# Experts' output rows: scattered to DRAM by token and choice and added once at the end, instead of added set by set through a one-hot product

## The chip, the cores and the metric

The kernel runs on one core of one Trainium2 chip. The core has TensorE (PE, matrix products into PSUM), VectorE (DVE), ScalarE (ACT), GpSimd (Pool) and SyncE (SP), each with its own queue of instructions, and 16 DMA engines that all queues share. The metric is the device time of one execution in microseconds; lower is better.

## The reference

Two blocks follow one another on 1024 tokens of 1024 features, all in float32. The first has three mixers (state space, pooling, gated spatial) and a gated feed-forward layer. The second has a convolution and a gated linear attention, a layer norm and a mixture of experts. Only the last part matters here:

```python
def hier_moe(x, w_rg, b_rg, w_re, b_re, w1, w3, w2):
    ...                                  # 8 groups of 8 experts: one group a token, two experts in it
    expert = g_sel * EXPERTS_PER_GROUP + top_i
    ...
    def expert_block(args):
        xb, e = args
        hdn = jax.nn.silu(xb @ w1[e]) * (xb @ w3[e])
        return hdn @ w2[e]
    ys = lax.map(expert_block, (xs, block_e)).reshape(n_slots, d) * slot_w[:, None]
    out = jnp.zeros((n_tok, d), x.dtype).at[slot_tok].add(ys)
```

and then `x = layer_norm(DEEPNORM_ALPHA * x + ffn, ln2_g, ln2_b)`. Every token has two experts out of 64, so 2048 rows are computed; an expert has three matrices of 1024 x 512 floats (2 MB each).

## The kernel before

Everything up to the router is not touched, except that the change puts some writes into the down projection of the first block (`for c0 in range(0, NF, 2)`, 11 steps of two hidden tiles, products `pd` on TensorE, L1099 their sums on VectorE; at `c0 == 2` four of the operand splits are on Pool).

`route` sorts the experts by load and gives every one a fixed number of rows (`CAP`): 256, 128, 64 or 32 by rank. The rows lie in 32 columns of 128 slots; half of the slots are empty. The tables it leaves are `xdx` (a slot's token, beyond the tokens for an empty one), `tokf` (the same as float) and `wtab` (its weight). On the way it has `ydx`, 2 x token + choice.

`experts` works through 30 sets of experts in the order `ORDER = "FQDPPQDPPQSSPQSQSPSQSPSPSPQSSQ"`. A set has one column (D two): S one expert with 128 rows, P two with 64, Q four with 32, F the first two with 64, D one expert with 256 rows in two columns. The matmul work of a column is the same for each kind; the weights are not: 6.3 MB for each expert.

- `weights` loads a set's matrices on SP's queue, 2 MB a load, into a ring of eight slots (`E.chunk`, L1918). A load waits until the slot's former content is read. For Q sets the third matrix comes in 16 loads of 0.5 MB (L1948).
- `fetch` gathers the rows of the next set from DRAM, an indirect DMA on Pool's queue (`take`, L1660); `turn` transposes them (`pxg`, L1965; ACT copies them to `xT`).
- `hidden` (L1978) makes gate and up products `pg` and `pu`, 8 k-steps; then silu on ACT and a multiplication on VectorE.
- `rows` transposes the result (`ph`, L1994; VectorE copies it to `hT`), multiplies by the third matrix (`py`, L2001) and writes the weighted rows as high and low parts `yh`, `yl` (L182, L183).
- `spread` (L2006) adds them to their tokens: VectorE makes a one-hot `S` of the rows' tokens (L2009), and for each of 8 tiles of 128 tokens TensorE makes four products `pa` (L2016, L2017), and VectorE adds two results of 128 x 512 to the residual `K.xa` (`xr`, L2021). These parts stand between the k-steps of the next set's `hidden` (`between`), so a column has 32 products and 16 additions.

After the last set `further` handles rows beyond an expert's own, a loop with a count read at run time, which runs zero times for this input. Then the layer norm of 8 tiles, with the last column's `spread` products and the residual summed in PSUM (L2016 to L2019). A scheduler places the instructions on each engine from the order of the code, by their dependences.

Of the kernel before, what the change touches and what calls it, by code (L numbers as in the profile page):

```python
# [18 lines left out]
P = 128  # L19
# [4 lines left out]
# Mixture of experts: rows for an expert by its rank in load; the first NFIX are not ranked.  # L24
# [4 lines left out]
NOVF = 40  # L29
LAST = "qpfpffff"  # L30
# [4 lines left out]
# The convolution's channel tiles that Pool takes.  # L35
# [23 lines left out]
def prep(a):  # L59
    """Host side: layout only."""  # L60
# [94 lines left out]
def helpers(tc, K):  # L155
    """Small closures shared by the phases."""
# [28 lines left out]
    def mm3(ps, l, r, k, n):  # L185
        """One 128-deep step of a float32 product out of split operands (hi, lo)."""
        pe.matmul(ps, l[0], r[0], start=(k == 0), stop=False)  # L187
        pe.matmul(ps, l[0], r[1], start=False, stop=False)  # L188
        pe.matmul(ps, l[1], r[0], start=False, stop=(k == n - 1))  # L189

    def rstd_of(out, ss, n, eps, tmp):
        """out = 1/sqrt(ss/n + eps)"""
# [9 lines left out]
    def wblock(src, alloc=WH, eng=()):  # L202
        """256 columns of a weight with 8 k-tiles: split operands per k."""
# [10 lines left out]
    def wtile(src):  # L214
        """128 columns of a weight with 8 k-tiles: split operands per k."""
# [14 lines left out]
class Operands:  # L230
    """The activations [k, token] as one side of Winograd's products: the blocks (1,1), (2,1) and (2,2) of 4 k-tiles and
    half of the tokens and the sums t1..t4 of blocks; lists of split k-tiles. The second half of the tokens comes by
    transposed(k), and build() makes what needs it, part by part; until then sums wait in eight more tiles (raw)."""
# [61 lines left out]
class Weights:  # L295
    """The operands out of two weight tiles (8 k-tiles, 128 columns), made one by one."""
# [27 lines left out]
def winograd(tc, H, B, M, sets, tick=lambda: None):  # L324
    """out = W^T X for two weight tiles after the other (sets), X in its operands B: seven products of 4 k-tiles, 128 columns
    and 512 tokens instead of eight. A set: srcs, the weight tiles; own: whether the result goes to tiles of its own or
    takes part in the former set's; post(i, n, c, r): what to do with quarter i of the result r (of weight tile n; c is its
    place in the tiles); done(tiles). The first two sets' products come in the order in which B is made."""
# [103 lines left out]
def s5_params(tc, K, alloc, s5, B1, Bs):  # L432
    """Discrete dynamics of the 24 groups; (re | im) of the 64 states stacked on 128 partitions."""
# [106 lines left out]
    # rotation by 8 tokens: unit part and its tables over 16 blocks and 8 x 16 blocks  # L540
# [28 lines left out]
    # input and output matrices  # L569
# [22 lines left out]
def front1(tc, I, K):  # L592
# [106 lines left out]
    def fill():  # L699
        """One tile of z_b or z_v, between the steps of the state space mixer."""  # L700
# [19 lines left out]
    def s5_in(b):  # L720
        """Input matrices, and the inputs of the blocks of 8 tokens taken to the end of the block."""
# [8 lines left out]
        # transposed input matrix, and its (im | -re) form  # L730
# [8 lines left out]
        # inputs of a block on partitions (token in block, channel)  # L739
# [9 lines left out]
        # cos and sin of the rotation of 0..127 blocks: 16 x (0..7) and 0..15  # L749
# [13 lines left out]
    def s5_state(b, o):  # L763
        """The states before the blocks, the block Toeplitz matrix of 8 tokens with the skip, the output matrices."""
# [83 lines left out]
    # pool mixer, among the tiles of v and u  # L848
# [42 lines left out]
    # layer norm of v  # L891
# [14 lines left out]
    # gated linear unit of the state space mixer  # L906
# [25 lines left out]
    # gated spatial mixer, as the last tiles of u arrive  # L932
# [52 lines left out]
    def norm(t, n, junk):  # L985
        """n = x1 / rms for a tile of tokens."""
# [29 lines left out]
    def op_tile(name):  # L1016
        """A half of an operand for the products (512 columns)."""
        nop[0] += 1
        if nop[0] % 5 in (1, 3) and not h2.raw:
            return F(name, (P, 512), F32R, tag="op", bufs=8)  # L1020
        return WH(name)
# [42 lines left out]

    for f in range(3):
        load(f, A4 if f < 2 else WR)
    for c0 in range(0, NF, 2):
        acts, wds = [], []
# [23 lines left out]
        for t in range(8):  # L1092
# [7 lines left out]
            if c0 == NF - 2:  # L1100
                # x1 / rms, in place
# [23 lines left out]
def front2(tc, I, K):  # L1125
# [33 lines left out]
    def tick(n=1):  # L1159
        """Emit some of the convolution's work between the steps of other work, for DVE and Pool at their rates."""  # L1160
# [7 lines left out]
    # the convolution, for tokens 2m and 2m + 1 out of U0 = u[2m..], U1 = u[2m + 1..], with taps a = w[0::2], b = w[1::2]:  # L1168
    # (a + b) * U1 + a * (U0 - U1) and (a + b) * U1 + b * (U0 shifted - U1)
# [1012 lines left out]
```

## Time and profile before

| | |
|---|---|
| median of three runs | 3346.24 us (3345.73 to 3349.76) |
| span of the profiled execution, first to last instruction | 3335.6 us |
| mean granted TensorE clock | 0.979 |
| TensorE / VectorE / ScalarE / Pool busy | 94% / 59% / 25% / 21% |
| DMA | 632.07 MB, mean 189 GB/s over the span |

Only the span and the runs' times are known of the executions; the profiled one's time outside its span is not shown, so the difference to the median, 10.6 us, is taken as what lies around a span. In the 40 slices of the page, 83.4 us each, the DMA engines are 0.1 to 0.5 busy until slice 25 and 0.5 to 0.9 from then on: that is the expert stage, 2165 to 3291 us. A row of a stretch gives for each engine its busy time and the number of instructions, then the granted clock (1.00 is 2.4 GHz, 0.50 is 1.2 GHz), the DMA engines' busy share and what they moved.

### The profile page before, as it was taken

Reading aid. Unit: us, or ns where it says so; the run is one execution under the profiler, and the core shown is the slowest. Engines: PE = TensorE matmul, PEld = TensorE weight load, DVE = VectorE, ACT = ScalarE, POOL = GpSimd, SP = SyncE. Lnnn points to the kernel's source line nnn. Section 1 sums busy time; section 2 is a strip of 40 time slices with the busy share of each in tenths; the row PEclk is TensorE's granted clock in tenths of the full one; section 3 lists DMA queues with packets and bytes.
Section 4 is the critical chain, followed back from the end, with each engine's and each line's share of the span. In section 5 each row is a group of like instructions: output and inputs, shape, how many; then the busy total and the mean of one; then the engine's idle time right before and its main releaser. Section 6 shows DMA issues by size and latency. Waiting matters only on the chain. (4 is left out here: it accounts for less than half of the span.)

```text
span 3335.6 us, 42339 instructions
## 1 busy us (share of the span) xinstructions
PE 3123.5 (94%) x16175; PEld 2205.2 (66%) x16175; DVE 1971.3 (59%) x3211; ACT 843.5 (25%) x1474; POOL 712.2 (21%) x545
## 2 busy tenths in 40 slices
PE   7889899999999899999899999899999999999996
PEld 7779878888887687778788789834343434444442
DVE  7774685555667999767895643644344333334435
ACT  4242433333112433344324421210000000001002
POOL 4530264332100433325421421010000000000001
PEclk9999999999999999999999999999999999999998
DMA  3012232223322322322213854397969999898795
GB/s 119 17 51 89 76 101 76 82 81 116 128 91 80 120 89 95 120 89 66 76 64 103 270 189 185 129 368 310 380 279 382 383 375 423 356 409 326 303 392 190
DMA packets 128061, 632.07 MB, mean 189 GB/s; under 512 B 16176, under 2 KB 29360, under 8 KB 107248
## 3 DMA queue, kind: packets, MB, share of 16 engines
q1 hardware_dynamic: 118384, 607.36, 48.0%
q0 software_dynamic: 7168, 17.79, 1.4%
q10 hardware_dynamic: 2304, 4.20, 0.3%
q8 instruction: 128, 2.10, 0.3%
q14 instruction: 77, 0.63, 0.1%
HBM read 575.81 MB, written 61.87 MB: 191 GB/s over the span
## 5 line engine op out<-in xcount | busy, mean ns | idle before, releaser
L2021 DVE TENSOR_TENSOR xr<-xr,pa 128x512 f32<-128x512 f32 x498 | 320.0, 683 | 322.9 <-PE pa L2017 322.8
L1978 PE MATMUL pg<-w,xT 128*32 128x512 f32 (+2 forms) x1056 | 294.3, 605 | 9.7 <-ACT xT L1966 7.3
L1978 PE MATMUL pu<-w,xT 128*32 128x512 f32 (+2 forms) x1056 | 288.7, 593 | 0.0
L2001 PE MATMUL py<-w,hT 128*32 128x512 f32 (+2 forms) x1056 | 251.4, 603 | 31.0 <-DVE hT L1996 31.0
L2016 PE MATMUL pa<-yh,S 128*128 128x512 f32 x512 | 264.3, 517 | 10.4 <-DVE xr L2021 7.5
L1660 POOL DMA_INDIRECT xg<-x_d,xdx x31 | 30.9, 995 | 968.9 <-PE pxg L1965 968.6
L2017 PE MATMUL pa<-yl,S 128*128 128x512 f32 x512 | 204.4, 400 | 0.1
L2016 PEld LDWEIGHTS pa<-yh,S 128*128 128x128 f32 x512 | 96.1, 188 | 159.7 <-issue 91.8
L1985 ACT ACTIVATE h<-pg 128x512 f32<-128x512 f32 x32 | 19.1, 597 | 684.9 <-PE pg L1978 684.9
L2001 PEld LDWEIGHTS py<-w,hT 128*32 128x32 f32 (+2 forms) x1056 | 84.3, 135 | 158.9 <-issue 116.6
L183 DVE SCALAR_TENSOR_TENSOR yl<-py,wtab,yh 128x512 fp32r<-128x512 f32 x64 | 47.2, 749 | 237.4 <-ACT yh L182 234.8
L1978 PEld LDWEIGHTS pu<-w,xT 128*32 128x32 f32 (+2 forms) x1056 | 87.5, 135 | 148.4 <-issue 147.6
L320 POOL TENSOR_TENSOR ws<-wr 128x512 f32<-128x512 f32 x74 | 116.6, 1580 | 271.9 <-DMA wr<-in_w2T_dram 160.1
L1099 DVE TENSOR_TENSOR x<-x,pd 128x512 f32<-128x512 f32 x176 | 117.9, 685 | 75.5 <-PE pd L189 74.7
L179 DVE TENSOR_TENSOR ol<-ws,oh 128x512 fp32r<-128x512 f32 x148 | 125.5, 848 | 46.0 <-ACT oh L178 39.6
L1978 PEld LDWEIGHTS pg<-w,xT 128*32 128x32 f32 (+2 forms) x1056 | 75.0, 133 | 98.4 <-issue 76.8
L178 ACT ACTIVATE oh<-ws 128x512 fp32r<-128x512 f32 x148 | 92.1, 626 | 142.0 <-PE pm L188 134.2
L2017 PEld LDWEIGHTS pa<-yl,S 128*128 128x128 f32 x512 | 96.5, 189 | 45.5 <-issue 34.1
L188 PE MATMUL pd<-wdl,aoh 128*128 128x512 f32 x320 | 123.6, 390 | 0.0
L189 PE MATMUL pd<-wdh,aol 128*128 128x512 f32 x320 | 123.3, 389 | 0.0
L187 PE MATMUL pd<-wdh,aoh 128*128 128x512 f32 x320 | 121.0, 394 | 0.1
L179 DVE TENSOR_TENSOR ol<-wr,oh 128x512 fp32r<-128x512 f32 x117 | 109.4, 936 | 7.3 <-ACT oh L178 5.1
(807 smaller groups left out, 8205.5 us busy)
## 6 DMA issues: line engine op xcount, KB each, us to landing
w<-in_we_dram SPq DMA_DIRECT2D x160, 2048.0 KB, 15.1
w<-in_we_dram SPq DMA_DIRECT2D x128, 512.0 KB, 10.2
wr<-in_w2T_dram SPq DMA_DIRECT2D x34, 512.0 KB, 3.7
wr<-in_wg_dram SPq DMA_DIRECT2D x22, 512.0 KB, 3.3
wr<-in_wu_dram SPq DMA_DIRECT2D x22, 512.0 KB, 4.0
act_d<-go SPq DMA_DIRECT2D x22, 512.0 KB, 2.9
wrD<-act_d SPq DMA_DIRECT2D x22, 512.0 KB, 3.4
wrD<-in_wd_dram SPq DMA_DIRECT2D x22, 512.0 KB, 4.1
```

The source lines that it names most:

```text
L178: act.activation(hi, src, AF.Copy)
L179: (eng or dve).tensor_tensor(lo, src, hi.bitcast(F32), op=OP.subtract)
L187: pe.matmul(ps, l[0], r[0], start=(k == 0), stop=False)
L188: pe.matmul(ps, l[0], r[1], start=False, stop=False)
L189: pe.matmul(ps, l[1], r[0], start=False, stop=(k == n - 1))
L320: self.pool.tensor_tensor(s, self.s[a], self.s[b], op=op)
L1099: dve.tensor_tensor(xs, xs, pd, op=OP.add)
L1978: pe.matmul(p[r], x[:, k, r], ws[k4][:, k % 4, j], start=(k == 0), stop=(k == 7))
L2001: pe.matmul(py[j][r], hT[:, k, r], ws[2][:, k, j], start=(k == 0), stop=(k == 3))
L2016: pe.matmul(pa, o, yh[:, j], start=True, stop=False)
L2017: pe.matmul(pa, o, yl[:, j], start=False, stop=not keep)
L2021: dve.tensor_tensor(x, x, pa, op=OP.add)
```

## The change

- In the first block's down projection, from `c0 == 4`, a DRAM table `y2d` of 2048 rows is filled with zeros, by eight DMAs of 1 MB on Pool's queue from a small zero tile.
- `route` keeps `ydx` for all columns.
- For the first 27 sets `rows` writes the weighted rows unsplit into one of two tiles `y0`, `y1`, and `put` scatters them to `y2d` by `ydx`, an indirect DMA on Pool's queue (rows without a token are beyond the bound and skipped). There is no `spread` for them.
- The last three sets (S, S, Q; `NLATE = 3`) go through `spread` as before, with `S`, `yh`, `yl` allocated later.
- Ahead of the last set's weights SP loads `y2d`, 1 MB for each tile of tokens, into four ring slots, and VectorE and Pool add both choices to the residual (`add`).
- `turn` for the next set is called after `hidden`, not at the start of the next set; `hT` is copied in two halves.

```diff
+def put(nc, K, y, ix):
+
+    nc.gpsimd.indirect_dma_start(out=K.y2d, out_offset=bass.IndirectOffsetOnAxis(ap=ix, axis=0), in_=y, in_offset=None,
+                                 bounds_check=2 * T - 1, oob_is_err=False)
...
+    K.y2d = tc.dram_tile([2 * T, D], F32, name="y2_d")
...
     for c0 in range(0, NF, 2):
+        if 4 <= c0 < 20:
+            i = (c0 - 4) // 2
+            if i == 0:
+                zero = F("zero", (P, 512))
+                pool.memset(zero, 0.0)
+            nc.gpsimd.dma_start(K.y2d[i * 256:(i + 1) * 256, :].rearrange("(p a) (b c) -> p (a b) c", p=P, c=512),
+                                zero[:, None, :].to_broadcast([P, 4, 512]))
...
-        dve.tensor_copy(hT, ph.rearrange("p (k t) -> p k t", k=4))
+        p4 = ph.rearrange("p (k t) -> p k t", k=4)
+        dve.tensor_copy(hT[:, 0:2], p4[:, 0:2])
+        dve.tensor_copy(hT[:, 2:4], p4[:, 2:4])
...
+        if len(R) == 1:
+            for j in range(2):
+                act.activation(R[0][:, hs[j]], py[j], AF.Copy, scale=w)
+            return
...
+    n_late = len(order) - NLATE
+    ys, n_y = [K.A4("y0"), K.A4("y1")], 0
+    S = K.A4("S", (P, 2, 512), F32R)
+
+    def add(c):
+
+        y = E.chunk().rearrange("p (t k d) -> p t k d", t=2, k=2)
+        for j in range(2):
+            t = 2 * c + j
+            nc.sync.dma_start(y[:, j], K.y2d[2 * t * P:2 * (t + 1) * P, :].rearrange("(p k) d -> p k d", k=2))
+        for j in range(2):
+            for k in range(2):
+                x = K.xa[2 * c + j]
+                (dve, pool)[j].tensor_tensor(x, x, y[:, j, k], op=OP.add)
+
     xs = K.xg
+    xT = [turn(x, PS) for x in xs]
     for i, rs in enumerate(order):
+        if i == len(order) - 1:
+            for c in range(4):
+                add(c)
         ws = weights(ids[i] if i < 2 else [expert_id(r) for r in rs], len(rs) in CUT)
...
-        xT = [turn(x, PT if i else PS) for x in xs]
...
+        if i == n_late:
+            R = [S] + [K.A4(n, (P, 2, 512), F32R) for n in ("yh", "yl")]
         h = hidden(xT, parts, nxt)
+        xT = [turn(x) for x in xs]
         for j, c in enumerate(cols(rs)):
-            rows(R, h[j], parts, col(K.wtab, c), *[nxt] * (j > 0))
-            nxt = spread(R, col(K.tokf, c))
+            if i < n_late:
+                y = ys[n_y % 2]
+                n_y += 1
+                rows([y], h[j], parts, col(K.wtab, c))
+                put(nc, K, y, col(K.ydx, c))
+            else:
+                rows(R, h[j], parts, col(K.wtab, c), *[nxt] * (j > 0))
+                nxt = spread(R, col(K.tokf, c))
```

What the scheduler makes of it is shown at three places. TensorE's queue from the end of the first P set's `hidden` on, before:

```order
L1994 MATMUL ph<-ident,h 128x128 x4
L2001 MATMUL py<-w,hT 64x512 x16
L1965 MATMUL pxg<-ident,xg_18945 128x128 x8
L1978 MATMUL pg<-w,xT_19262 64x512 x2
L1978 MATMUL pu<-w,xT_19262 64x512 x2
L2016 MATMUL pa<-yh,S 128x512
L2017 MATMUL pa<-yl,S 128x512
L2016 MATMUL pa<-yh,S 128x512
L2017 MATMUL pa<-yl,S 128x512
```

and the same place after the change:

```order
L1984 MATMUL pxg<-ident,xg_18956 128x128 x8
L2013 MATMUL ph<-ident,h 128x128 x4
L1997 MATMUL pg<-w,xT_19273 64x512
L2022 MATMUL py<-w,hT 64x512 x16
L1997 MATMUL pg<-w,xT_19273 64x512
L1997 MATMUL pu<-w,xT_19273 64x512 x2
L1997 MATMUL pg<-w,xT_19273 64x512 x2
L1997 MATMUL pu<-w,xT_19273 64x512 x2
L1997 MATMUL pg<-w,xT_19273 64x512 x2
```

The four `pa` products after each k-step are gone, the next but one set's transposes `pxg` stand ahead of `ph` or later in the next `hidden`, and here the next set's first product `pg` stands ahead of the third matrix's products `py`.

Pool's queue at the end of the expert stage, before (`xg` are the gathered rows of a set, the two numbers its two buffers):

```order
L1660 DMA xg_19261<-x_d,xdx 128x1024
L1660 DMA xg_18945<-x_d,xdx 128x1024
L2044 TENSOR_LOAD nblk
L2045 COMPARE_AND_BRANCH
L2045 ISA
L2045 UNCONDITIONAL_BRANCH
```

and after (`y_d` is the table in DRAM, `ydx` the slots' rows in it, `xr<-xr,w` the additions of the loaded table):

```order
L1672 DMA xg_19272<-x_d,xdx 128x1024
L1672 DMA xg_18956<-x_d,xdx 128x1024
L1678 DMA y_d<-y_19313,ydx 2048x1024
L1678 DMA y_d<-y_19312,ydx 2048x1024
L2102 TENSOR_TENSOR xr<-xr,w 128x1024 x8
L2069 TENSOR_LOAD nblk
L2070 COMPARE_AND_BRANCH
```

Between gathers stand scatters, two and two; the last two are those of sets 25 and 26, and the two gathers ahead of them are those of sets 28 and 29.

SP's queue ahead of the last set's weights, before (`perm` holds the experts by rank; each load of weights has an address computed from it):

```order
L2036 TENSOR_LOAD perm
L2036 ISA x2
L2036 TENSOR_LOAD perm
L2036 ISA x2
L1918 ISA
L1918 DMA w<-in_we_dram 128x4096
L1918 ISA
```

and after:

```order
L1937 DMA w<-in_we_dram 128x4096
L1937 ISA
L1937 DMA w<-in_we_dram 128x4096
L2098 DMA w<-y_d 128x2048 x8
L2061 TENSOR_LOAD perm
L2061 ISA x2
```

The eight loads of the table stand between the weights of set 28 and those of set 29; the first of them waits for the scatters.

## Rows read from the trace of the kernel before

**Rows 1.** Busy time by stretch: us, engines (instructions), clock, DMA share, GB/s; expert stage.

```profile
2169.00:3291.00 1122.00, 1064.30 (x4583) 463.60 (x4579) 441.39 (x707) 96.15 (x160) 37.45 (x41) 1.00 0.88 358
```

**Rows 2.** Waits from 2150 us on: engine, tile, releaser: us, times, longest.

```profile
PE pg L1978 <- DMA w<-in_we_dram: 2.4, 4, 1.2
```

**Rows 3.** Waits of SP's queue from 2150 us on.

```profile
SPq L1918 <- PE pu L1978: 458.0, 48, 19.2
```

**Rows 4.** Order of time on PE, one P set: start, us, what, times [idle before].

```profile
2337.63 7.09 PE L2001 MATMUL py<-w,hT 128*64 128x512 f32 x32 [1.11 <-DVE hT L1996]
2344.65 1.09 PE L1965 MATMUL pxg<-ident,xg 128*128 128x128 f32 x8
2346.02 1.08 PE L1978 MATMUL pg<-w,xT 128*64 128x512 f32 x4 [0.28 <-ACT xT L1966]
2346.93 1.03 PE L1978 MATMUL pu<-w,xT 128*64 128x512 f32 x4
2347.88 0.50 PE L2016 MATMUL pa<-yh,S 128*128 128x512 f32 x1
...
2349.01 1.08 PE L1978 MATMUL pg<-w,xT 128*64 128x512 f32 x4
...
2369.87 0.60 PE L1994 MATMUL ph<-ident,h 128*128 128x128 f32 x4
2371.59 1.94 PE L2001 MATMUL py<-w,hT 128*64 128x512 f32 x8 [1.12 <-DVE hT L1996]
```

**Rows 5.** Busy time by stretch, instructions of tile `pa` alone (PE, PEld, DVE, ACT).

```profile
2169.00:3291.00 1122.00, 332.88 (x992) 172.78 (x992) 318.73 (x496) 0.00 (x0) 1.00 0.88 358
```

**Rows 6.** Busy time by stretch of 25 us in the expert stage.

```profile
2175.00:2200.00 25.00, 23.16 (x121) 9.42 (x117) 12.62 (x42) 4.37 (x5) 7.18 (x11) 1.00 1.01 428
2300.00:2325.00 25.00, 24.73 (x97) 12.45 (x97) 15.03 (x24) 2.24 (x4) 0.99 (x1) 1.00 0.30 104
2375.00:2400.00 25.00, 24.23 (x127) 8.97 (x124) 9.89 (x15) 2.35 (x4) 0.99 (x1) 1.00 0.96 362
2575.00:2600.00 25.00, 21.98 (x145) 7.79 (x144) 5.77 (x10) 2.95 (x5) 0.99 (x1) 1.00 1.02 419
3200.00:3225.00 25.00, 23.47 (x73) 12.53 (x72) 11.06 (x17) 2.95 (x5) 0.00 (x0) 1.00 1.00 426
```

**Rows 7.** Loads of weights on SP's queue: count, ns min/median/max, first and last start.

```profile
L1918 SPq DMA_DIRECT2D w<-in_we_dram x155: 332/333/821, 2169.0 to 3251.4; - x155
...
L1948 SPq DMA_DIRECT2D w<-in_we_dram x128: 332/333/1192, 2222.7 to 3278.2; - x128
...
DMA to landing us min/median/max: 4.0/11.0/39.8
```

**Rows 8.** The gathers (line 1660): count, ns of issue, and time to landing.

```profile
L1660 POOL DMA_INDIRECT xg<-x_d,xdx x31: 988/988/1106, 2185.0 to 3185.6; - x31
...
DMA to landing us min/median/max: 3.4/10.8/13.6
```

**Rows 9.** Instructions on tile `xr` in the final norm, 128 x 1024.

```profile
L2112 DVE SCALAR_TENSOR_TENSOR xr<-xr,znf,w x5: 1275/1275/3432, 3304.6 to 3328.4; 128x1024 f32<-128x1024 f32 x5
...
L2110 POOL TENSOR_TENSOR xr<-xr,w x3: 2347/2368/2377, 3304.6 to 3321.3; 128x1024 f32<-128x1024 f32 x3
```

**Rows 10.** Busy time by stretch: the down projection of the first block.

```profile
860.00:1060.00 200.00, 199.92 (x875) 162.74 (x875) 136.57 (x185) 35.83 (x36) 0.94 (x1) 1.00 0.28 92
```

**Rows 11.** Busy time by stretch of 2 us, around an idle TensorE.

```profile
2152.00:2154.00 2.00, 0.00 (x0) 0.00 (x0) 1.90 (x8) 0.00 (x0) 0.00 (x0) 0.64 1.07 451
...
2166.00:2168.00 2.00, 2.00 (x10) 1.57 (x10) 1.83 (x8) 0.88 (x2) 0.00 (x0) 0.50 0.02 4
2170.00:2172.00 2.00, 2.00 (x12) 0.63 (x10) 1.93 (x3) 0.00 (x0) 0.55 (x1) 1.00 1.05 238
```

**Rows 12.** Order of time on PE, end of the last set and start of the tail.

```profile
3283.41 7.81 PE L2001 MATMUL py<-w,hT 128*32 128x512 f32 x64 [0.79 <-DVE hT L1996]
3293.41 0.50 PE L2016 MATMUL pa<-yh,S 128*128 128x512 f32 x1 [2.19 <-DVEq L2045]
```

More of the change, by code (lines that the diff above doesn't have):

```diff
@@ L29 @@
 NOVF = 40
+NLATE = 3
 LAST = "qpfpffff"
@@ L1063, in load @@
             nc.sync.dma_start(raw[-1], src)
+    K.y2d = tc.dram_tile([2 * T, D], F32, name="y2_d")
+    zero = None
     for f in range(3):
@@ L1757, in route, with token_of @@
     xd0 = N((P, 1), I32)
-    def token_of(pt, dst):
+    def token_of(pt, dst, ydx=None):
         emp = ts(pt, 0.0, 8192.0, OP.is_equal, OP.mult)
-        ydx = N(pt.shape, I32)
+        ydx = N(pt.shape, I32) if ydx is None else ydx
         dve.scalar_tensor_tensor(ydx, emp, -1.0, pt, op0=OP.add, op1=OP.add)
@@ L1854, in route @@
     xdx = K.xdx = RT("xdx", (P, NC_), I32)
-    token_of(pt[:, :NC_], xdx)
+    K.ydx = RT("ydx", (P, NC_), I32)
+    token_of(pt[:, :NC_], xdx, K.ydx)
     tokf = K.tokf = RT("tokf", (P, NC_))
@@ L1930, in experts @@
     xg, xTs = K.xg + [K.A4("xg1")], [K.xT0, K.A4("xT1", (P, 8, P))]
-    R = [K.A4(n, (P, 2, 512), F32R) for n in ("S", "yh", "yl")]
+    R = None
     hs = [slice(0, 512), slice(512, 1024)]
```

## The prediction

> **What bounds the kernel now.** I read the views in this order. First the expert stage as one stretch, from the first weight load of the second set to the last product of the last set [rows 1]: TensorE works 1064 of 1122 us at full clock, the DMA engines 0.88 of it, and they move 358 GB/s, that is 401.7 MB. Then the waits in that stage [rows 2, 3]: PE waited for weights 2.4 us in all, while SP's queue waited 458 us for PE to give up a ring slot. So PE sets the pace there and the loads follow it. Then what PE does in one set of kind P [rows 4]: from one `py` to the next 33.96 us, and inside `hidden` each of 8 k-steps takes 2.99 us (2346.02 to 2349.01), of which 1.27 us (2347.74, when the 1.72 us of gate and up products are through, to 2349.01) are four products of `spread`. In the whole stage the products of `spread` (tile `pa`) are busy 333 us, overlaps counted [rows 5]. The change takes most of these away.
>
> What comes next is the DMA: in 20 of the 25-us stretches of the stage its share is at or above 1.00, and these stretches move 393 to 428 GB/s, 422 in the mean (the first, a slower one and the last in [rows 6]). In others it stands: 104 GB/s at 2300 [rows 6], with the ring full. Removing PE work turns that standing time into loading, until the loads are the bound.
>
> **Part 1, `spread` leaves 29 of 32 columns.** A P set without it: 33.96 - 8 x 1.27 = 23.8 us. The end of `hidden` then no longer has a spread product between the last `pu` and the transposes `ph`, so the silu and the multiplication show: +1 us, 24.8. All kinds have the same matmul work per column (128 weight columns, 512 moving), so 32 columns take 32 x 24.8 = 794 us, and two spreads that stay inside the stage add some 17: **811 us of PE work**, against 1122 before. PE alone would end the stage 310 us earlier. It will not, since the weights cannot come that fast.
>
> **Part 2, what the DMA must move.** Weights after 2169.05: 155 loads of 2.097 MB and 128 of 0.524 MB [rows 7] are 392.2 MB. Gathers: 2048 rows of 4 KB less those of set 0, 8.1 MB. New: scatters of the rows of 29 columns, at most as many bytes, 7.8 MB (rows without a token are skipped, as in the gathers). New: the sum's eight loads of `y2d`, 1 MB each on SP's queue, ahead of the last set's weights: 8.4 MB. Sum 416.5 MB. At 422 GB/s: **987 us**. This is more than the 811 of PE, so the stage becomes DMA-bound. At 428 it is 973, at 410 (the rate of a stretch with the small `w2` loads, near [rows 6]) 1016.
>
> **Part 3, when the DMA still stands.** The ring holds 8 loads of 2.1 MB, 39.8 us at that rate. A Q set (12 loads, 59.6 us, 24.8 us of PE) leaves PE waiting; an S set (14.9 against 24.8) lets the loads run ahead; P takes 29.8 against 24.8. I followed the order of the sets with these numbers: a load starts when its slot's last reader is through, PE when its load is in. The lead that S runs build up stays under the ring's 39.8 us; only the two P P pairs ask for slots early, twice 4.7 us: **9 us**.
>
> The loads of `y2d` wait on SP for the last scatter (set 26), and behind them on SP stand all weights of the last set. Two 14.9-us sets of weights are still to come through when that scatter lands (a gather takes 10.8 us [rows 8] and I take the same for a scatter), so 0; if it were late, each us of it stands in full. DVE takes the eight additions of 1.28 us and Pool eight of 2.37 us [rows 9]; behind them on DVE stand additions of `spread` for set 27, which PE needs for its PSUM banks. The first pair of loads lands before PE is there, so 0 to 5 us, I take 0.
>
> **Part 4, the queues.** On Pool a scatter waits for ACT's scaled rows and the gathers of later sets stand behind it. In Pool's order a gather is issued about a set and a half ahead of its use, 30 us or more against 10.8 to land [rows 8]; issue 1.0 us each. Cost 0; without that cover 10 us a set. ACT keeps its two scaled copies a column (now whole rows instead of high parts), DVE loses 19 instructions in each of 29 columns; neither is the bound.
>
> **Part 5, the zeroing** of `y2d` before: eight loads' worth of 1 MB writes on Pool's queue while the down projection runs with PE at 199.92 of 200 us and DMA at 0.28 [rows 10]. 8.4 MB are 20 us of DMA time in free space. But two of them and a memset stand among four splits on Pool that PE needs about 1 us after they end: 0 to 10 us, I take 2.
>
> **Part 6, TensorE's clock.** PE will now wait for weights some 175 us in all (987 less 811). After an idle gap the granted clock fell to 0.64 and 0.50 (the 1.2 GHz level) and was back at 1.00 about 4 us after dense work began [rows 11]. What is lost is half of some 4 us per long wait, and only where PE is then late for a slot or at the end: 0 to 20 us, I take 5 in the stage and 2 in the tail.
>
> **The sum.** 2169 + 987 + 9 + 5 = 3170. The last load lands 2.8 us after its bytes are due (4.0 us is the shortest landing of 0.5 MB [rows 7], less 1.2 of moving), and two products follow: 3174. From the end of the last product (3283.41 + 7.81 = 3291.2 [rows 12]) to the end of the span are 44.4 us that do not change: 3218.4; with 2 for the zeroing and 2 for the tail's clock 3222.4. The median of the runs is 10.6 us above the span (3346.2 against 3335.6): **3233 us**, 3.4% faster.
>
> **Rivals.** (a) *The DMA runs at its best*: 428 GB/s with no standing and no loss of clock: 2169 + 973 + 4 + 44.4 + 10.6 = 3201. For it: all full stretches without small loads are at 426 to 428. Against: a quarter of the bytes are not.
>
> (b) *PE stays the bound, at a low clock.* The loads give PE 987 / 32 = 30.8 us a column; it needs 24.8 at full clock. If it ran over a quarter of its work at 1.2 GHz, it would be late again. At 35%, 33.5 us a column: 2169 + 33.5 x 32 + 17 = 3258 at the last product, +44.4 + 10.6 = 3313. [...] Against: between waits PE has solid work of 7 to 14 us, and a late PE has no waits.
>
> (c) *The mixed traffic is slower, and the result is slower than before.* In one mechanism: gathers and scatters of single rows hold the DMA engines without moving as much, and the flow falls towards what the stage shows at a share of 0.96 with a gather in flight, 362 GB/s in the stretch at 2375 [rows 6]. Then 416.5 / 0.362 = 1151 us, the end 2169 + 1151 + 4 + 44.4 + 10.6 = 3379. It decides from 379 GB/s downwards (416.5 MB in the 1100 us that leave the span as it was). Against: the stretch at 2575 holds a gather too and moves 419 [rows 6].
>
> (d) *It does not do what it says*: PE's order has, at some sets, the first product of the next `hidden` ahead of `py`, so that PE could stand for a weight with `w2` slots unreleased behind it, and the loads with it. If 10 us went that way in every other set, the gain would be used up: about 3345.
>
> (e) *The DMA is at its limit already*: the stage's mean of 358 GB/s [rows 1] is what the memory gives, and the new 16.2 MB come on top: 416.5 / 0.358 = 1163 us, the end 3391. Against: the full stretches move 426 and 428 [rows 6], and those that stand do so with SP waiting for PE [rows 3]. The Trainium skill, "DMA: Bandwidth & Descriptors", section Specifications, has a line that gives one core about 358 GB/s of HBM, and another that puts the fabric's ceiling at 435. With the first as a limit the change could only lose; the trace disagrees with it (a full stretch is a fifth above) and agrees with the second.
>
> **How the numbers follow.** Forecast 0.72, (a) 0.10, (b) 0.10, (c) 0.04, (d) 0.03, (e) 0.01. A measurement of this kernel tells about 0.2% from no change. Faster: 0.72 + 0.10 + 0.09 = 0.91; same 0.03 (most of (d)); slower: (c), (e) and 0.01 of (b), 0.06. The range runs from (a) at 3198 to 3283, which is the forecast with 410 GB/s (+29), 15 more for the clock and 6 for zeroing; (a) and half of (b) are inside.
>
> **What would show it.** Right: in the expert stage DMA share near 1.00 throughout at 415 to 425 GB/s, PE waiting for `w` some 150 to 200 us, PE busy near 810; the stage's last product near 3174; 44 us of tail. Wrong: stretches with a DMA share under 0.9 (SP waiting for PE as now, or for a scatter), PE's granted clock under 1.00 over many stretches, or full shares at under 400 GB/s. If the down projection's end moves by over 5 us, Part 5 was mis-sized.

## The result, and the profile after

The changed kernel takes **3249.39 us** (median of four runs, 3245.66 to 3250.73) against 3345.98 us before (median of four runs): ratio **0.9708**, interval 0.9694 to 0.9722, so 2.9% faster. Forecast were 3233 us and a range of 3198 to 3283. The profiled execution took 3248.72 us, with a span of 3246.8.

The expert stage and the tail, as rows of stretches that answer to [rows 1] (engines as there: PE, PEld, DVE, ACT, Pool; then granted clock, DMA share, GB/s):

```profile
2175.00:3200.70 1025.70, 904.73 (x3655) 343.63 (x3651) 106.03 (x198) 100.41 (x160) 90.12 (x78) 0.96 0.98 407
3200.70:3247.00 46.30, 21.29 (x61) 12.11 (x60) 35.55 (x79) 19.47 (x46) 15.52 (x6) 0.75 0.29 114
```

The share of the DMA engines rose from 0.88 to 0.98 and their rate from 358 to 407 GB/s, while TensorE fell from 95% busy to 88%: the bound has changed hands. The products `pa` of `spread` in the stage, against [rows 5], and what the stage moved, by queue (q1 is SP's, q0 Pool's):

```profile
2175.00:3200.70 1025.70, 22.33 (x64) 10.70 (x64) 20.98 (x32) 0.00 (x0) 0.96 0.98 407
```
```profile
DMA packets 50588, 417.28 MB, mean 407 GB/s; under 512 B 9367, under 2 KB 9367, under 8 KB 29680
...
q1 hardware_dynamic: 41904, 400.57, 94.0%
q0 software_dynamic: 8640, 16.11, 4.1%
```

Of 333 us of `pa` 22 are left. The waits of TensorE and of SP's queue from 2150 on (in total, times, longest; us), which answer to [rows 2, 3]:

```profile
PE pg L1997 <- DMA w<-in_we_dram: 76.6, 29, 4.6
PE ph L2013 <- DVE h L2005: 19.6, 23, 0.9
...
SPq L1937 <- PE pu L1997: 246.7, 49, 16.4
SPq L1937 <- PE py L2022: 233.5, 49, 16.5
...
SPq L1967 <- PE pu L1997: 92.5, 16, 21.8
...
SPq L1937 <- DVE xr L2102: 16.7, 4, 9.7
...
SPq L2098 <- DMA y_d<-y,ydx: 13.7, 1, 13.7
```

TensorE now waits for weights (2.4 us before). SP's queue still waits for slots of the ring, for `pu` 247 us and no longer 458. For `py`, a wait that [rows 3] leave out, it is much as before:

```profile
SPq L1918 <- PE py L2001: 223.5, 32, 9.9
```

So SP waiting for TensorE does not mean that the DMA stands: with loads already in its queue the DMA works on. Two waits are new, for the last scatter (L2098) and for the additions of `y2d` that hold ring slots (L2102).

Where the DMA still stands is seen in stretches of 12.5 us. Out of the 82 that fill the stage, 68 have a share of 0.99 or more; they move 421.9 GB/s in the mean. These are the ones that lose most, in order of time, and a full one last:

```profile
2287.70:2300.20 12.50, 12.50 (x34) 5.47 (x34) 1.11 (x4) 1.37 (x2) 0.99 (x1) 1.00 0.90 381
2300.20:2312.70 12.50, 12.50 (x52) 4.31 (x53) 0.00 (x0) 1.37 (x2) 0.96 (x1) 1.00 0.70 240
2437.70:2450.20 12.50, 12.50 (x35) 5.25 (x33) 0.76 (x2) 1.80 (x3) 1.00 (x1) 1.00 0.76 316
2450.20:2462.70 12.50, 12.50 (x58) 4.21 (x58) 0.00 (x0) 0.95 (x2) 0.97 (x1) 1.00 0.90 341
2850.20:2862.70 12.50, 7.72 (x28) 1.58 (x29) 0.00 (x0) 0.00 (x0) 0.00 (x0) 0.59 0.89 334
3012.70:3025.20 12.50, 12.50 (x57) 4.93 (x57) 0.00 (x0) 2.46 (x4) 2.02 (x2) 1.00 0.84 334
3062.70:3075.20 12.50, 9.72 (x69) 2.84 (x72) 1.44 (x3) 0.60 (x1) 0.00 (x0) 0.97 0.80 280
3162.70:3175.20 12.50, 11.88 (x78) 3.77 (x76) 4.36 (x7) 0.00 (x0) 0.00 (x0) 1.00 0.57 237
3187.70:3200.20 12.50, 12.27 (x44) 3.24 (x42) 0.00 (x0) 0.30 (x1) 0.00 (x0) 1.00 0.81 321
...
2550.20:2562.70 12.50, 12.50 (x30) 5.51 (x29) 0.00 (x0) 0.00 (x0) 0.00 (x0) 1.00 1.01 429
```

Each loses 12.5 us times what its share lacks: the first four, which are the two P P pairs, 9.3 us; the four from 3012 on 12.3 us; all 82 together 25.6 us. In the first four TensorE is busy throughout and the loads wait for it. At 2850 and 3062 it is not: there a Q set is at work.

The sum of the prediction against this execution, in us:

| term | forecast | measured |
|---|---|---|
| first weights of the second set issued | 2169 + 2 | 2175.2 |
| bytes at the full rate | 987 (416.5 MB at 422) | 989 (417.3 MB at 421.9) |
| the DMA stands | 9 | 25.6 |
| low clock, slow short loads, last landing | 9 | 10.9 (what is left over; not measured term by term) |
| stage's last product | 3174 | 3200.7 |
| tail | 44.4 + 2 | 46.1 |
| around the span | 10.6 | 1.9 |

### The profile page after: what moved, and what is told of

It is laid out like the page before. It is cut to its first block, busy times and chain, and to the rows that moved or that the text cites. A ratio compares the mean times of both kernels' runs of the same rounds, so it can differ in the third digit from the quotient of the medians.

```text
span 3246.8 us, 39751 instructions
## 1 busy us (share of the span) xinstructions
PE 2970.0 (91%) x15247; PEld 2090.4 (64%) x15247; DVE 1635.0 (50%) x2700; ACT 847.3 (26%) x1474; POOL 768.1 (24%) x591
## 5 line engine op out<-in xcount | busy, mean ns | idle before, releaser
L2005 DVE TENSOR_TENSOR h<-h,pu 128x512 f32<-128x512 f32 x32 | 22.0, 687 | 842.5 <-PE pu L1997 842.5
L1997 PE MATMUL pg<-w,xT 128*32 128x512 f32 (+2 forms) x1056 | 348.8, 633 | 76.7 <-DMA w<-in_we_dram 76.6
L1997 PE MATMUL pu<-w,xT 128*32 128x512 f32 (+2 forms) x1056 | 342.9, 622 | 0.0
L2022 PE MATMUL py<-w,hT 128*32 128x512 f32 (+2 forms) x1056 | 281.9, 599 | 15.5 <-issue 12.4
L1997 PEld LDWEIGHTS pg<-w,xT 128*32 128x32 f32 (+2 forms) x1056 | 96.0, 139 | 244.1 <-issue 128.3
L1678 POOL DMA_INDIRECT y_d<-y,ydx x29 | 29.0, 999 | 433.5 <-ACT y L2026 433.5
L179 ACT ACTIVATE oh<-wr 128x512 fp32r<-128x512 f32 x117 | 72.9, 625 | 118.9 <-PE pm L189 110.0
L180 POOL TENSOR_TENSOR wl<-wrB,wh 128x512 fp32r<-128x512 f32 x40 | 60.0, 1522 | 181.8 <-ACT wh L179 181.8
L1213 DVE SCALAR_TENSOR_TENSOR cadve<-cadve,vec 128x512 f32<-128x512 f32 x105 | 102.1, 972 | 0.1
L1213 DVE SCALAR_TENSOR_TENSOR cudve<-cudve,vec 128x512 f32<-128x512 f32 x105 | 98.2, 936 | 0.8
## 6 DMA issues: line engine op xcount, KB each, us to landing
w<-in_we_dram SPq DMA_DIRECT2D x160, 2048.0 KB, 23.9
```

What stands on the lines that cost most here:

```text
L179: act.activation(hi, src, AF.Copy)
L180: (eng or dve).tensor_tensor(lo, src, hi.bitcast(F32), op=OP.subtract)
L1213: dve.scalar_tensor_tensor(o, x, w, c, op0=OP.mult, op1=OP.add)
L1678: nc.gpsimd.indirect_dma_start(out=K.y2d, out_offset=bass.IndirectOffsetOnAxis(ap=ix, axis=0), in_=y, in_offset=None, bounds_check=2 * T - ...
L1997: pe.matmul(p[r], x[:, k, r], ws[k4][:, k % 4, j], start=(k == 0), stop=(k == 7))
L2022: pe.matmul(py[j][r], hT[:, k, r], ws[2][:, k, j], start=(k == 0), stop=(k == 3))
```

## The experiments

All ratios are to runs of the kernel before that were taken beside the runs in question; the changed kernel's is 0.9708, and 0.001 is 3.3 us.

**What the bytes cost.** Two kernels leave traffic out. One is without `put(nc, K, y, col(K.ydx, c))`:

> The 29 scatters are left out; zeroing, the eight loads of y2d and the additions stay (so the sum adds zeros). Theory A, the DMA engines bound the stage: 7.8 MB less at the 407 GB/s that the stage of the changed kernel moves are 19 us, and the wait of 13.7 us of SP for the last scatter goes too, of which some is covered: 3249 - 19 to - 30, 3219 to 3230. Rival B, TensorE bounds the stage at its lowered clock (0.96 in the mean, 905 us busy): no bytes matter, 3246 to 3252. Rival C, the single rows of the scatters hold the DMA engines beyond their bytes: more than 35 us are gained, under 3214.

Measured: 3225.04 us, ratio 0.9644 (0.9627 to 0.9660), 21 us less. Its stage lasts 1004.8 us (2172.7 to 3177.5), 20.7 less, at the same 407 GB/s; 7.8 MB at the full rate are 18.5. Theory A holds, and B (TensorE at a low clock sets the pace) and C (rows cost more than bytes) fall. The wait of 13.7 us for the last scatter, gone here, is worth some 2 us by these stages.

The other is without zeroing, scatters, loads and additions:

```diff
-        if 4 <= c0 < 20:
...
-        if i == len(order) - 1:
-            for c in range(4):
-                add(c)
...
-                put(nc, K, y, col(K.ydx, c))
```

> Zeroing, scatters, loads of y2d and their additions are all left out; 29 columns then reach no token, and only the removal of their one-hot products is left. Theory A: 16.2 MB less in the stage at 407 GB/s are 40 us, the standing at the stage's end (13.7 us for the scatter, the shares of 0.79 and 0.88 after 3150) goes for some 10 more, the zeroing is worth 1 to 3: 3249 - 50 = 3199 (3192 to 3210). Rival B (TensorE at a low clock): 3243 to 3252. If the zeroing is what put the whole front 6 us later, the first weight load of the second set is issued near 2169 here and not at 2175; if that is the spread between executions, it stands between 2167 and 2177 without a pattern.

Measured: 3207.47 us, ratio 0.9600 (0.9584 to 0.9616): 36 us less by the ratios, not 50, at the upper end of A's range. Against the run before, 8.4 MB of `y2d` bring only 16.6 us of stage (988.2 against 1004.8) and not the 20 of their bytes, and nothing of the standing at the end goes. Two of its rows show why, the end of set 28 and the first half of the last Q set:

```profile
3106.30:3118.80 12.50, 12.50 (x42) 5.21 (x41) 3.70 (x7) 2.46 (x4) 0.00 (x0) 1.00 0.76 300
3118.80:3131.30 12.50, 12.19 (x69) 3.94 (x68) 5.14 (x8) 0.00 (x0) 0.00 (x0) 1.00 0.39 155
```

TensorE is busy, the last set's `w2` can be issued from 3129.4 on only, when that first half, with the spread of set 28 in it, has given up slots, and the DMA stands for 10.6 us. In the changed kernel (5.4 us there) the loads of `y2d` come before and push the weights back; that they fill part of such a time is argued from this and not shown.

On zeroing: the first load of the stage's first block is issued at 2139.8 here, 2143.3 and 2142.3 in two further kernels without zeroing (below) and 2139.9 before; in the ten profiles with zeroing between 2140.1 and 2152.0, 2144.2 in the mean, against 2141.3. The 6 us of the changed kernel's profile are mostly the spread between executions (12 us among the ten); the zeroing is about 3 in the mean, which so wide a spread shows roughly at best.

**More or fewer late sets.**

```diff
-NLATE = 3
+NLATE = 6
...
-        if i == len(order) - 1:
-            for c in range(4):
-                add(c)
+        if i >= len(order) - 4:
+            add(i - len(order) + 4)
```

> Six sets instead of three keep the one-hot product, and the loads of y2d come one pair ahead of each of the last four sets instead of all ahead of the last. Theory A: TensorE's three further spreads (31 us) are covered by its waits of some 120 us, 0.8 MB of scatters less are 2 us, and the standing at the end (13.7 us of SP behind the last scatter, shares of 0.79 and 0.88 in 3150 to 3200, 8 us) goes: 3249 - 10 = 3239 (3234 to 3245). Rival B: three spreads at 10 us each stand in full, 3270 to 3282. Rival D, the standing at the end was covered by the lead of the loads: 3246 to 3250.

Measured: 3265.04 us, ratio 0.9772 (0.9756 to 0.9789): 21 us slower, between the ranges of A and B. Up to 2994 it runs as the changed kernel; then:

```profile
3015.00:3040.00 25.00, 23.96 (x95) 10.04 (x95) 12.08 (x18) 2.28 (x4) 2.46 (x3) 1.00 0.76 297
3065.00:3090.00 25.00, 22.98 (x154) 7.22 (x151) 1.44 (x3) 1.79 (x3) 0.00 (x0) 1.00 0.81 303
3165.00:3190.00 25.00, 23.81 (x101) 8.32 (x100) 11.18 (x17) 1.37 (x2) 0.00 (x0) 1.00 0.57 213
```

TensorE is at 92 to 96% at full clock and the DMA stands: 44.7 us of standing in the whole stage (2169.0 to 3213.9) against 25.6. My theory that the spare 120 us of TensorE cover the spreads falls: some two thirds of the three spreads (31 us) stand in full. In the P and S sets a full ring waits for TensorE. And a spread in a Q set is no better covered: set 26, which stands 2.5 us in the changed kernel (the row of 3062 there), has the spread of set 25 in the first half of its products here, and stands 8.0:

```profile
3056.50:3069.00 12.50, 12.00 (x78) 4.22 (x80) 5.19 (x8) 0.00 (x0) 0.00 (x0) 1.00 0.36 152
```

The run changes two things, the number of late sets and the place of `y2d`'s loads, and does not tell what the second is worth.

**TensorE's work itself.** Half of `py` is left out:

```diff
-        for k in range(4):
+        for k in range(0, 4, 2):
```

> Half of the products py is left out (k-tiles 1 and 3 of w2; its loads all stay), so TensorE has 3.5 us less in each of 32 columns, 112 us in all, and the DMA moves the same bytes. Theory A, the loads set the pace and TensorE only delays them where it gives up a slot late (25 us of standing in the stage: 9 at the two P P pairs, 12 after 3012, the rest elsewhere): 10 to 22 us are gained, ratio to before 0.964 to 0.968. Rival B, TensorE at its lowered clock sets the pace in most of the stage: 60 us or more are gained, ratio under 0.953. Rival F, the standing comes from the DMA side itself (the short loads of w2 at its k-tiles, landing times): within 4 us of the changed kernel, ratio 0.9695 to 0.972.

Measured: 3238.73 us, ratio 0.9686 (0.9669 to 0.9704): 7 us for 112 us of work. TensorE is busy 809.7 us and its clock is 0.91:

```profile
2174.50:3194.80 1020.30, 809.66 (x3127) 299.09 (x3123) 104.11 (x196) 99.54 (x160) 88.18 (x78) 0.91 0.99 408
3162.00:3174.50 12.50, 12.18 (x85) 4.18 (x85) 4.08 (x7) 0.00 (x0) 0.00 (x0) 1.00 0.15 61
```

B falls for the stage as a whole. A is right in kind, a little under its range: standing goes from 25.6 to 21.6 us only, since the last Q set alone now loses 10.6 us (share 0.15). In that set the first eight loads are issued by 3151 and have landed by about 3165 (share 0.05 from there to 3170); its `w2` needs the slots of its own first loads, free only at 3173 when the first half of its k-steps, in which set 28's spread stands, is nearly through. Until then nothing is left to load. Half of `py` less does not help there.

**Is it the place of the Q set?** The last S and Q are exchanged:

```diff
-ORDER = "FQDPPQDPPQSSPQSQSPSQSPSPSPQSSQ"
+ORDER = "FQDPPQDPPQSSPQSQSPSQSPSPSPQSQS"
...
-        ws = weights(ids[i] if i < 2 else [expert_id(r) for r in rs], len(rs) in CUT)
+        ws = weights(ids[i] if i < 2 else [expert_id(r) for r in rs], len(rs) in CUT or i == len(order) - 1)
```

> The changed kernel with the last S and the last Q set exchanged (order ends Q S instead of S Q) and the last set's w2 loaded k-tile by k-tile. In the changed kernel the loads stand about 12 us after 3012, 8 of them in the last Q set, which needs twelve loads of a ring of eight, so that its last loads wait for its own first half. Theory L, this chain of the last Q set is what stands at the end: with it out of the last place 5 to 10 us are gained, ratio to before 0.9675 to 0.9695. Theory M, the standing comes from the three one-hot products in the last sets wherever Q stands, or is given back as the last set's h now waits on DVE behind the additions of y2d: ratio 0.970 to 0.974. Of no effect, ratio 0.9695 to 0.971, if the last loads' landing bounds both.

Measured: 3264.63 us, ratio 0.9767 (0.9752 to 0.9783), 20 us slower and outside all three ranges. The standing went along with the Q set (share 0.57 in the 12.5 us from 3123). But that set's first half holds a spread here too, set 27's, so this run does not tell L's chain from M's one-hot products. Nothing is gained, because the last set's weights now come behind `y2d`'s, land some 23 us after issue, and TensorE's whole last column, with the spread of the set before, stands after them:

```profile
PE pg L1997 <- SPq L2070: 22.9, 1, 22.9
```

(the wait is put down to SP's queue; the two loads it needs were issued from 3163.4 on). So theory L is wrong on the worth; on the cause see the next runs.

**`y2d` off SP's queue.** Its loads go by Pool's queue into tiles of their own, beside the last set's weights, and DVE adds:

```diff
-        y = E.chunk().rearrange("p (t k d) -> p t k d", t=2, k=2)
...
+        for k in range(2):
+            y = K.A4("ya")
+            nc.gpsimd.dma_start(y, K.y2d[2 * t * P:2 * (t + 1) * P, :].rearrange("(p k) d -> p k d", k=2)[:, k])
+            x = K.xa[t]
+            dve.tensor_tensor(x, x, y, op=OP.add)
```

with one late set, with two, and with one and most additions behind the last set's `hidden`:

> One set keeps the one-hot product instead of three; y2d is loaded by 16 transfers of 0.5 MB on Pool's queue into tiles of their own, beside the last set's weights on SP and not ahead of them; DVE alone adds. Theory A, what stands at the end is TensorE's work in the two S sets with spread (2 x 9 us) and SP's queue behind y2d (13.7 and 16.7 us, partly covered): 8 to 14 us are gained, ratio 0.9665 to 0.9685. Rival H, the last scatter comes so late (about 3142) that with four or five tiles and 11 us of landing the additions end 14 us after the last set's hidden needs DVE: ratio 0.971 to 0.976.

> The same with two sets that keep the one-hot product. Theory A: one spread less on TensorE (9 us) and SP free of y2d: 5 to 12 us gained, ratio 0.967 to 0.9695. Rival H does not hold here (the last scatter at about 3112 leaves 60 us). If the standing at the end is not TensorE's and SP's doing: ratio 0.970 to 0.972.

> One set with the one-hot product and y2d loaded on Pool's queue as in the run before, but only the first three tokens' tiles are added ahead of the last set's hidden on DVE; the next three behind its hT, the last two on Pool. Where all sixteen additions stood ahead of it, TensorE waited 32.5 us for h of the last set, and the kernel was 4 us slower than the changed one. Theory A: without that wait the last product is bound by the last weights (about 3184 against 3200); the additions come in pairs every 5.1 us (four tiles in flight), end about 3191 and hold the last split back by some 7 us: 4 to 10 us gained, ratio 0.967 to 0.9695. If the last set's loads themselves come later (y2d's 8.4 MB beside them): ratio 0.970 to 0.973.

Measured: 3253.71 us, ratio 0.9735 (0.9715 to 0.9755); 3278.47, 0.9801 (0.9779 to 0.9822); 3243.14, 0.9710 (0.9689 to 0.9732). The first two put a new wait in the place of the old ones, since DVE's queue has the additions ahead of what TensorE needs. In the first it is `h` of the last set, in the second the additions of `spread` that free PSUM: a wait on DVE there too, which I had ruled out, and a time outside all ranges:

```profile
PE ph L2013 <- DVE h L2005: 33.3, 2, 32.5
```
```profile
PE pa L2041 <- DVE xr L2046: 36.6, 4, 14.4
```

In the third that wait is 8.1 us, and the kernel is as fast as the changed one: two spreads less on TensorE and both of SP's waits gone bring nothing that these runs can tell, as its second alternative had it. Its stage (2170.0 to 3191.9) stands 23.9 us. None of them lie in the first half of the last Q set, in which no spread stands now; its `w2` is issued from 3138.8 on, and the DMA is full up to 3181:

```profile
3144.00:3156.50 12.50, 7.54 (x44) 1.93 (x45) 2.34 (x2) 0.00 (x0) 2.77 (x5) 0.86 1.02 408
3156.50:3169.00 12.50, 4.05 (x20) 1.31 (x15) 5.95 (x8) 0.60 (x1) 3.22 (x6) 0.81 1.03 409
3169.00:3181.50 12.50, 10.23 (x44) 2.15 (x44) 6.91 (x8) 0.00 (x0) 2.15 (x4) 0.92 1.02 408
```

`y2d`'s 8.4 MB now share the DMA with the last weights, whose loads land 20.4 us after issue in the median, and 6.8 us stand in the last 9.4 us of the stage, while the last loads come in. So the loads of the last sets still set the end.

**Who adds.** All sixteen additions on DVE:

> All sixteen additions of y2d on DVE, none on Pool. In the changed kernel eight on DVE beside eight on Pool took 2.37 and 3.0 us each instead of 1.28 and 2.37. If the two engines slow each other, sixteen on DVE alone take 16 x 1.28 = 20.4 us instead of about 30 (3121 to 3151), the last set's loads wait less for their slots, and up to 9 us are gained: 3241 to 3247. If the additions are slow for another reason (the DMA's writes), they take 16 x 2.4 = 38 us on DVE and the kernel is 5 to 10 us slower, 3254 to 3259. If their end hides behind other work: 3249 within 2.

Measured: 3250.73 us, ratio 0.9722 (0.9706 to 0.9739): no difference that these runs can tell. The additions (first line in this kernel, then the two of the changed one: min/median/max ns, first and last start):

```profile
L2102 DVE TENSOR_TENSOR xr<-xr,w x16: 1211/1216/1224, 3128.2 to 3156.4; 128x1024 f32<-128x1024 f32 x16
```
```profile
L2102 POOL TENSOR_TENSOR xr<-xr,w x8: 2357/3001/3327, 3121.7 to 3144.9; 128x1024 f32<-128x1024 f32 x8
L2102 DVE TENSOR_TENSOR xr<-xr,w x8: 1211/2702/3431, 3124.2 to 3150.4; 128x1024 f32<-128x1024 f32 x8
```

Side by side each engine is slowed by the other; alone, DVE takes sixteen in 29 us as well, its other work between them.

**The two edits on the side**, the earlier `turn` and `hT` in halves. First with every set on the one-hot product and no table, then the moved `turn` alone in the kernel before, then both undone in the changed kernel:

```diff
-        xT = [turn(x, PT if i else PS) for x in xs]
...
         h = hidden(xT, parts, nxt)
+        xT = [turn(x) for x in xs]
```

> Every set keeps its one-hot product, nothing is scattered, zeroed or loaded back: of the change only the earlier turn of the next set's rows and the copy of hT in halves are left. Theory A: TensorE is dense before, so both give nothing beyond the gaps of some 0.5 us a column at ph and py: ratio 0.995 to 1.002. Rival G, a good part of the gain comes from these two edits (a gap of 1 to 2 us less in each of 32 columns): ratio under 0.993.

> The kernel before with one edit, the turn of the next set's rows moved behind hidden, hT copied whole as before. It splits the 26 us that the two edits cost together when every set keeps its one-hot product. If the moved turn is the cause (it puts the next set's first products of pg and pu among those of py, and the loads' slots come free in another order): ratio 1.006 to 1.011. If the halves of hT are the cause: ratio 0.998 to 1.003.

> The changed kernel with the turn of the next set's rows back at its old place (head of the loop, after the weights) and hT copied whole again. With every set on the one-hot product these two edits cost 26 us (ratio 1.0082). Theory I, they cost only where TensorE is the bound, and the loads hide them now: within 4 us of the changed kernel, ratio 0.9695 to 0.972. Theory J, they cost in every set and undoing them gives back 10 to 26 us: ratio 0.963 to 0.968. Theory K, with the old place a TensorE without spread waits for ACT's copy of the turned rows at each set's head (1.1 us of pxg and some 0.3 to 1 us of wait in 32 columns, and 0.8 us more at hT): 10 us or more lost, ratio above 0.974.

Measured: 3370.52 us, ratio 1.0082 (1.0061 to 1.0104), outside both ranges; 3369.80, 1.0088 (1.0064 to 1.0112); 3247.62, 0.9713 (0.9696 to 0.9730). The moved `turn` costs 29 us where TensorE is the bound, `hT` in halves nothing that these runs can tell, and in the changed kernel both cost nothing. TensorE in the kernel before with the moved `turn`, at the end of the first P set (start, duration, products):

```profile
2346.97 1.08 PE L1978 MATMUL pg<-w,xT 128*64 128x512 f32 x4
2347.88 0.59 PE L1978 MATMUL pu<-w,xT 128*64 128x512 f32 x1
2347.96 0.64 PE L2001 MATMUL py<-w,hT 128*64 128x512 f32 x1
...
2356.26 1.07 PE L1978 MATMUL pg<-w,xT 128*64 128x512 f32 x2
```

Four such instructions run in 1.08 us where the two experts' stand together; torn apart by others, two take 1.07. Once its rows are turned, the next set's products are ready early, and the scheduler mixes them with `py` and `pa`. TensorE is busy 41 us more in the stage than before (1105.7 us against 1064.3 in [rows 1]):

```profile
2171.40:3320.00 1148.60, 1105.69 (x4573) 478.46 (x4571) 443.78 (x707) 99.28 (x159) 42.84 (x41) 0.99 0.87 349
```

By groups `pg` and `pu` gain 33 us in the sets of two experts and 20 in those of four, and 1 in those of one, whose products fill the array and have nothing to be torn from. The changed kernel has the same (first fence, busy us and mean ns) and the one with both edits undone has not (second):

```profile
L1997 PE MATMUL pg<-w,xT 128*64 128x512 f32 x318 | 115.5, 601 | 0.0
L1997 PE MATMUL pu<-w,xT 128*64 128x512 f32 x320 | 114.9, 597 | 0.0
```
```profile
L1997 PE MATMUL pu<-w,xT 128*64 128x512 f32 x320 | 87.8, 595 | 0.0
L1997 PE MATMUL pg<-w,xT 128*64 128x512 f32 x318 | 86.9, 599 | 3.8 <-ACT xT L1985 3.8
```

55 us more in these two groups, which overlap: TensorE as a whole is busy 904.7 us against 886.1 in the stage, 19 us more, at the same total time: theory I. The Trainium skill, "TensorEngine Tiling (Array Packing)", section Key Properties, says that tiles of the array can load weights and multiply in parallel, independently of one another; the rows agree, and add that the order decides whether they get to.

No version beat the changed kernel while doing all of its work: three are level with it (additions on DVE, `turn` back, `y2d` on Pool's queue with the additions split).

## Why the prediction was right, and where its sizes were off

**Right.** The bound moved from TensorE to the loads, by the bytes of Part 2: 417.3 MB measured for 416.5, full stretches at 421.9 GB/s for 422, and leaving 7.8 MB out gives 20.7 us for the 18.5 of their bytes. The two P P pairs stand 9.3 us for the 9 of Part 3. Queues on Pool cost next to nothing (Part 4): scatters land 10.7 us after issue, as taken, and TensorE waits for gathered rows once, 4.1 us. The tail is 46.1 for 46.4, its clock low at first as forecast (0.65 from 3204 to 3208, where the kernel before has 1.00 at that place of its tail).

**Right in the sum, not in a step.** Part 3 took the last scatter to be in time, and each us of its lateness to stand in full. SP did wait 13.7 us for it, and next to nothing of that stood: the stretches from 3087.7 to 3162.7 have shares of 1.00 to 1.03, since loads already issued kept the DMA full, and taking the wait away (without scatters; with `y2d` on Pool's queue) brings some 2 us or nothing.

**The step that was mis-sized: the rest of Part 3, standing of 9 us, measured 25.6.** I followed the ring and found only the P P pairs asking for slots early, and I counted the two late spreads inside the stage as 17 us of covered TensorE work. Left out was that a Q set needs twelve loads of a ring of eight, so that its `w2` cannot be issued until its own first half is multiplied, and that a spread that stands in this half puts that off. The last Q set of the changed kernel (TensorE, and at the end SP's queue):

```profile
3150.11 1.05 PE L1997 MATMUL pg<-w,xT 128*32 128x512 f32 x2
3151.94 0.50 PE L2041 MATMUL pa<-yh,S 128*128 128x512 f32 x1
...
3167.45 0.39 PE L2042 MATMUL pa<-yl,S 128*128 128x512 f32 x1
3167.78 1.07 PE L1997 MATMUL pg<-w,xT 128*32 128x512 f32 x8
...
3174.02 14.91 SPq L1967 DMA_DIRECT2D w<-in_we_dram  x16
```

From its first product to its first load of `w2` 24 us go by, 16 of them between the first and the last `pa`; by 3170 the other loads are in (share 0.11 from there to 3175), and 5.4 us stand. It takes both, the ring and the spread: where no spread stands in that half the last Q set does not hold the loads up (one late set, third run), and set 26 loses 2.5 us without a spread and 8.0 with one (six late sets). In both runs the loads of `y2d` lie elsewhere too, so the share of each is not exact. The other standing after 3012 is not the spreads' doing, whose first `pa` is at 3117: 2.0 us at 3012, in a P set behind an S set with TensorE busy throughout, 2.5 in set 26 and 2.4 at 3187, when the last loads come in. The remaining 4 us are scattered, 1.4 of them at 2850.

**Two terms outside the stage, of opposite sign.** The front is 6 us later, not 2: zeroing is about 3 in the mean, the rest the spread of executions. And 10.6 us around the span were no such thing: 1.9 us lie around a span. The profiled execution of before (3335.6) was a faster one than the three timed runs: later runs of that kernel go down to 3337.18. So 8.7 us that do not exist stood in for part of the standing: that the forecast missed the time by only 16 us is in part luck, without them it would have been 3224, 25 us low.

**The signs.** Of those that I named for being right, the tail and the rate of the full stretches came; the waits for weights (76.6 us, not 150 to 200), TensorE's busy time and the stage's last product (3200.7, not 3174) did not. Of those for being wrong, seven of the 82 stretches have a share under 0.9, and 24 a clock under 1.00. **Part 1** gave 811 us of TensorE work; it is busy 905, at a mean clock of 0.96 and with products torn apart by the moved `turn` (19 us), to which I gave no price at all; the rest was not taken apart. It matters little behind the loads: 112 us less of its work bring 7. What the low clock of **Part 6** costs was not measured by itself. The lower end of the range is called (a) at 3198, but (a)'s own sum is 3201.

**The rivals.** (a), no standing at all, and (b), TensorE bound at a low clock, were the wrong way out on either side; TensorE is the bound locally, in the late sets, but there at full clock. (c) and (e) fall by the rate: stretches full of weights, gathers and scatters move 422, and those without scatters 421.4. (d), next products ahead of `py`, is in the rows, and undoing it in the changed kernel brings nothing; the 29 us that the moved `turn` costs in the kernel before come with 41 us more of busy TensorE, and not by (d)'s way, a TensorE that stands for weights (8.2 us there, 2.4 before).

## What to carry to other kernels

When work is taken off the bound, sum what the next bound has to do at the rate of its own full stretches, and then look for where it will stand: a ring of buffers makes a set wait for itself as soon as the set needs more slots than the ring has, and any other work that stands in the part that frees the slots lengthens this wait. Spare time of an engine is not a pool to draw on; it covers new work only if it lies where the work is put. And an edit that only moves instructions should be priced with the old bound in mind: it may cost 29 us there and nothing here.

## What the runs showed of the hardware

- Additions of 128 x 1024 floats with both inputs in SBUF, on DVE and Pool at once: 2.70 and 3.00 us in the median, against 1.22 (sixteen on DVE alone) and 2.37 ([rows 9]) alone. Eight of each took 29.9 us (3121.7 to 3151.6), with DVE's other work between them, sixteen on DVE alone 29.4 (3128.2 to 3157.6), with the same kind of work between: the two engines together gained nothing here. The Trainium skill, "SBUF — State Buffer", section SBUF: two separate sides, says that DVE with two SBUF inputs and Pool share a port pair under an exclusive lock, so that one blocks for the other's whole instruction; these rows agree: the longest took 3.43 and 3.33 us, and one after the other the two would take 3.59.
- An indirect scatter of up to 128 rows of 4 KB takes Pool 1.0 us and lands in 10.7 beside full weight loads, the same as the gathers; on the DMA engines it costs about its bytes (7.8 MB left out gave 20.7 us, 18.5 at the full rate).
- 2 MB loads land 23.9 us after issue in the changed kernel, with the DMA engines at 0.98 in the stage, and 15.1 before, at 0.88. The load that is needed first is late too: with S and Q exchanged the last set's first two, issued from 3163.4 on behind `y2d`'s, landed 22.2 to 24.6 us later.
